# Batched matrix product on one core: transposes in two pieces a half, and two-bank copies in the last group

## The chip, the cores and the metric

The kernel runs on one core of one Trainium2 chip. The time is that of one execution on the device in microseconds (us); less is better. The engines that matter are TensorE (PE, the matrix products; PEld is its weight load), VectorE (DVE), ScalarE (ACT), GpSimd (POOL) and SyncE (SP), which here only issues transfers. The transfers themselves run on 16 DMA engines.

## The reference

```
x: 32 x 256 x 512, y: 32 x 512 x 384, float32
out[b] = x[b] @ y[b]          # 32 products of 256x512 by 512x384, float32 out
```

## The kernel before

**Groups and halves.** The 32 batches are taken four at a time (Q = 4), which makes N = 8 groups, numbered 0 to 7. Each of the four batches of a group has 32 of the 128 partitions (PQ = 32). x of a group is loaded as `x_sb` (two buffers), y as `y_sb` (two buffers). The 256 rows of a product are cut into two halves (NE = 2, index e) of 128 rows, and the sum over the 512 columns of x into T = 16 steps of 32. A chunk is STEP = 4 of these steps, so a half has NC = 4 chunks.

**SP** issues all transfers in one queue (lines 75 and 98 to 111). Two groups are loaded at once at the start; after that x of group n waits until POOL has cast both halves of group n - 2, and y of group n until POOL has cast the first half of x of group n - 1 (`s_cast`). The output of all groups stays in `o_sb` and goes out by three stores at the end: groups 0 to 4 (issued behind the last load, when group 5 is in its second half), groups 5 and 6 (when group 7's second half has done its first chunk), and group 7, which waits for ACT's and DVE's last copies (lines 107 to 109).

**POOL** casts to 16 bit, x a half at a time into `x_r` (`round_x`, line 121) and y in pieces into `y_r` (`round_y`, line 130). `x_r` and `y_r` have one buffer each. The cast of a half of x of group n waits until DVE has done with the half that it overwrites, which DVE tells with the first of its copies (`s_free`). The cast of a piece of y waits until TensorE has used up that piece of the group before.

**DVE** transposes `x_r` into `xt_sb`, which holds one half (`transpose_x`, line 154: 128 partitions x 256 words for a chunk, each word two 16-bit values). While TensorE computes half (n, e), DVE transposes the next half, chunk by chunk, each as soon as TensorE has used up the same chunk (`chunk_done`, lines 174 to 179). Then it copies 5 of the 16 blocks of the finished half from the accumulators to `o_sb` (`collect`, line 163; a block is 32 partitions x 384 elements, for one batch g and one of H = 4 runs of 32 rows). The loop runs over groups 0 to 6; group 7 is written out behind it (lines 189 to 191).

**ACT** copies the other 11 blocks of each half, bank after bank, each as soon as the bank's last product is done (`scalar_half`, line 195). Groups 0 to 5 are a loop, groups 6 and 7 (STRAIGHT = 2) are written out.

**TensorE** takes, for each half, one token each from `s_act` and `s_dve` (the accumulators of two halves ago are copied out; two tokens of each are there at the start), and at each chunk one from `s_yr` and one from `s_xt`. It then issues 16 products a chunk, 64 a half (lines 231 to 250). The accumulators `o_ps` are 8 PSUM banks, one for each half and batch: bank e x 4 + g.

Of the kernel before, what the change touches and what calls it, by code (L numbers as in the profile page):

```python
# [11 lines left out]
Q = 4  # L12
NE = 2
STEP = 4
STRAIGHT = 2
# [4 lines left out]
def kernel(  # L20
# [9 lines left out]
    _, _, K = y.shape  # L30

    PQ = P // Q
    R = I // PQ
    H = R // NE
    T = J // PQ
    TW = T // 2
    N = B // Q
    NC = T // STEP

    def sbuf(name, shape, dtype):  # L40
        return nc.alloc_sbuf_tensor(name, shape, dtype).ap()
# [3 lines left out]
    o_sb = sbuf("o_sb", [P, N, NE, H, K], F32)  # L45
# [4 lines left out]
    o_ps = nc.alloc_psum_tensor("o_ps", [P, NE * Q, 512], F32).ap()  # L50
# [7 lines left out]
    s_act = nc.alloc_semaphore("s_act")  # L58
    s_dve = nc.alloc_semaphore("s_dve")
    s_pe = nc.alloc_semaphore("s_pe")  # L60
# [24 lines left out]
    def bank_done(n, e, g):  # L85
        return (n * NE + e) * MARKS + NC + g

    def chunk_done(n, e, a):
        return (n * NE + e) * MARKS + (a + 1 if a < NC - 1 else MARKS)
# [57 lines left out]


    v = nc.vector
    AW = STEP // 2  # L150
    words = x_r.bitcast(F32).rearrange("p e h (q t) -> p e t h q", t=TW)
    xt_w = xt_sb.rearrange("p t (h s) -> p t h s", s=PQ)

    def transpose_x(e, a):
        w = slice(a * AW, (a + 1) * AW)
        v.transpose(xt_w[:, w], words[:, e, w]).then_inc(s_xt, 1)  # L156
# [3 lines left out]
    BLOCKS = [(g, h) for g in range(Q) for h in range(H)]  # L160
    OWN = 5

    def collect(copy, n, e, blocks, first=None, last=None):
        for i, (g, h) in enumerate(blocks):
            ins = copy(  # L165
                o_sb[g * PQ : (g + 1) * PQ, n, e, h],
                o_ps[h * PQ : (h + 1) * PQ, e * Q + g, :K],
            )
            if i == 0 and first is not None:
                ins.then_inc(first, 1)  # L170
            if i == len(blocks) - 1 and last is not None:
                ins.then_inc(last, 1)

    def vector_half(n, e):
        for a in range(NC):
            v.wait_ge(s_pe, chunk_done(n, e, a))
            if a == 0:
                v.wait_ge(s_cast, NE * n + e + 2)
            transpose_x(1 - e, a)
        collect(v.tensor_copy, n, e, BLOCKS[-OWN:], s_free, s_dve)  # L180

    v.sem_inc(s_dve, NE)
    v.wait_ge(s_cast, 1)
    for a in range(NC):
        transpose_x(0, a)
    with v.Fori(0, N - 1) as n:
        for e in range(NE):
            vector_half(n, e)
    vector_half(N - 1, 0)
    v.wait_ge(s_pe, chunk_done(N - 1, 1, NC - 1))  # L190
    collect(v.tensor_copy, N - 1, 1, BLOCKS[-OWN:], None, s_dve)

    a_ = nc.scalar

    def scalar_half(n, e):
        for g in range(Q - 1):
            a_.wait_ge(s_pe, bank_done(n, e, g))
            blocks = [b for b in BLOCKS[:-OWN] if b[0] == g]
            collect(a_.copy, n, e, blocks, None, s_act if g == Q - 2 else None)
# [4 lines left out]
    with a_.Fori(0, N - STRAIGHT) as n:  # L204
        with a_.Fori(0, NE) as e:
            scalar_half(n, e)
    for n in range(N - STRAIGHT, N):
        for e in range(NE):
            scalar_half(n, e)

    te = nc.tensor

    def take(sem):
        te.wait_op(sem, 1, "sem-ge").then_inc(sem, -1)  # L214

    def product(ps, w, m, start, stop, g):
        return te.add_instruction(  # L217
            mybir.InstMatmult(
                name=nc.get_next_instruction_name(),
                start_tensor_calc=start,  # L220
                stop_tensor_calc=stop,
                tile_size=(PQ, P),
                tile_position=(PQ * g, 0),
                engine=mybir.EngineType.PE,
                ins=[te.lower_ap(m), te.lower_ap(w)],
                outs=[te.lower_ap(ps)],
            )
        )

    xt = xt_sb.bitcast(MM_DT).rearrange("p t (m c) -> p t m c", c=2)  # L230
    with te.Fori(0, N):
        with te.Fori(0, NE) as e:
            take(s_act)
            take(s_dve)
            for t in range(T):
                if t % STEP == 0:
                    take(s_yr)
                    take(s_xt)
                for g in range(Q):
                    s = slice(g * PQ, (g + 1) * PQ)  # L240
                    ins = product(
                        o_ps[:, e * Q + g, :K],
                        xt[s, t // 2, :, t % 2],
                        y_r[s, t],
                        t == 0,
                        t == T - 1,
                        g,
                    )
                    if t == T - 1 or (g == Q - 1 and t % STEP == STEP - 1):
                        ins.then_inc(s_pe, 1)  # L250
# [30 lines left out]
```

## Time and profile before

| What | us |
|---|---|
| median of three runs | 132.0 (131.89 to 132.18) |
| the profiled execution's own time | 132.13 |
| its span, first to last instruction | 130.8 |
| busy in the span: PE, PEld | 61.4, 46.7 |
| busy in the span: DVE, ACT, POOL | 82.7, 84.1, 74.2 |

The profiled execution took 1.3 us more than its span, which lies before the first instruction and behind the last one. HBM was read for 41.94 MB and written for 12.58 MB.

How to read the views quoted below. A row of groups has the line, engine, operation, out<-in with shapes and count, then busy us and mean ns of one, then the idle time ahead of it and what ended most of that. A row of the timeline has start and length in us, the engine, the line, the operation and a count; consecutive instructions of one kind are merged, and the idle time ahead of the first stands in brackets. SPq rows are issues of transfers. A row of stretches has the stretch, its length, the busy time and instruction count of PE, PEld, DVE, ACT and POOL, then the clock granted to TensorE, the mean share of 16 DMA engines and GB/s. A row of issues has the count, KB each and the time from issue to landing. In the row of DMA slices each digit is the busy share of one of 40 equal slices in tenths, 9 for 90% or more. A row of waits has total us, count and the longest.

### The profile page before, as it was taken

The numbers are of one execution on the slowest core, as the hardware profiler recorded it, in microseconds if no ns is written. First come the engines' busy times: TensorE is split into PE (matmuls) and PEld (weight loads), VectorE is DVE, ScalarE is ACT, GpSimd is POOL, SyncE is SP. The second block draws the span as 40 slices with busy tenths as digits, with TensorE's granted clock in tenths as the row PEclk, the third lists the DMA queues.
The fourth block names the chain that finished last, engine by engine and source line by source line (L and its number), as shares of the span: only waits on it lengthen the run. The fifth ranks groups of instructions, "written<-read, shape, count | busy, mean of one in ns | idle before, by whom it ended". The sixth has DMA issues, their size and how long they took to land. (4 is left out here: it accounts for less than half of the span.)

```text
span 130.8 us, 3199 instructions
## 1 busy us (share of the span) xinstructions
PE 61.4 (47%) x1024; PEld 46.7 (36%) x1024; DVE 82.7 (63%) x144; ACT 84.1 (64%) x178; POOL 74.2 (57%) x42
## 2 busy tenths in 40 slices
PE   0000009910992589089329905980975499100000
PEld 0000009800991566046129604970953236000000
DVE  0000036899379999985997997599999957920000
ACT  0400000599659989993998899399999957994000
POOL 0006991199929965992899459758973970000000
PEclk9999999995589689977986985599599959965555
DMA  5999999999999999999999999999999999999995
GB/s 120 451 396 441 421 431 451 443 408 428 451 413 421 438 443 401 436 436 443 423 458 398 443 408 466 398 418 436 463 398 408 427 438 425 436 428 421 425 440 248
DMA packets 3379, 54.55 MB, mean 417 GB/s; under 512 B 304, under 2 KB 304, under 8 KB 304
## 3 DMA queue, kind: packets, MB, share of 16 engines
q1 hardware_dynamic: 3376, 54.53, 98.1%
q14 instruction: 3, 0.02, 0.0%
HBM read 41.94 MB, written 12.58 MB: 417 GB/s over the span
## 5 line engine op out<-in xcount | busy, mean ns | idle before, releaser
L165 ACT COPY o_sb<-o_ps (+1 forms) x176 | 82.6, 469 | 31.7 <-PE o_ps L217 29.6
L217 PE MATMUL o_ps<-y_r,xt_sb 32*128 32x384 f16 x1024 | 61.4, 384 | 50.4 <-PEq L214 49.5
L217 PEld LDWEIGHTS o_ps<-y_r,xt_sb 32*128 32x128 f16 x1024 | 46.7, 107 | 64.6 <-issue 56.8
L156 DVE STREAM_TRANSPOSE xt_sb<-x_r 128x256 f32<-128x256 f32 x64 | 38.1, 626 | 30.9 <-POOL x_r L126 18.4
L136 POOL CAST y_r<-y_sb 128x1536 f16<-128x1536 f32 (+1 forms) x22 | 44.3, 2049 | 15.8 <-DMA y_sb<-in_y_dram 15.3
L165 DVE COPY o_sb<-o_ps 32x384 f32 (+1 forms) x80 | 44.6, 557 | 1.6
L126 POOL CAST x_r<-x_sb 128x2048 f16<-128x2048 f32 x16 | 30.2, 1893 | 16.8 <-DVE o_sb L165 12.1
L202 ACT ACT_TABLE_LOAD x1 | 1.3, 1283 | 3.4 <-PEq L78 3.4
L265 POOL MEMSET const-float32-0.0<- 128x1 f32 x1 | 0.1, 98 | 0.2 <-issue 0.2
L202 ACT COPY spare<-const-float32-0.0 1x1 f32<-1x1 f32 x1 | 0.2, 190 | 0.0
L265 POOL MEMSET const-bfloat16-1.0<- 128x1 bf16 x1 | 0.1, 101 | 0.0
L265 POOL MEMSET const-uint8-127<- 128x1 uint8 x1 | 0.1, 101 | 0.0
L265 POOL MEMSET const-float32-1.0<- 128x1 f32 x1 | 0.1, 98 | 0.0
## 6 DMA issues: line engine op xcount, KB each, us to landing
y_sb<-in_y_dram SPq DMA_DIRECT2D x8, 3072.0 KB, 16.8
x_sb<-in_x_dram SPq DMA_DIRECT2D x8, 2048.0 KB, 17.0
out_dram<-o_sb SPq DMA_DIRECT2D x1, 7680.0 KB, 33.9
out_dram<-o_sb SPq DMA_DIRECT2D x1, 3072.0 KB, 17.3
out_dram<-o_sb SPq DMA_DIRECT2D x1, 1536.0 KB, 11.5
```

The source lines that it names most:

```text
L126: po.tensor_copy(x_r[:, e], x_sb[n % 2][:, e * H : (e + 1) * H]).then_inc(s_cast, 1)
L136: ins = po.tensor_copy(y_r[:, s], y_sb[n % 2][:, s])
L156: v.transpose(xt_w[:, w], words[:, e, w]).then_inc(s_xt, 1)
L165: ins = copy(o_sb[g * PQ : (g + 1) * PQ, n, e, h], o_ps[h * PQ : (h + 1) * PQ, e * Q + g, :K],)
L202: a_.copy(spare, nc.const_aps.tensor(0.0, [1, 1], F32))
L217: return te.add_instruction(mybir.InstMatmult(name=nc.get_next_instruction_name(), start_tensor_calc=start, stop_tensor_calc=stop, tile_si ...
L265: nc = _bacc.Bacc("TRN2", target_bir_lowering=False, num_devices=1)
```

## The change

The transposes of a half are made in PT = 2 pieces of two chunks each (AW is doubled), so a piece waits for the second of its two chunks, and TensorE takes `s_xt` twice a half instead of four times. The accumulators change places: bank g x 2 + e instead of e x 4 + g, so the two halves of one batch lie in neighbouring banks. In group 7, ACT and DVE copy a block of both halves by one instruction (`collect_last`), when the second half's bank is done; the copies of group 7's first half that ran while the second half was computed are gone. ACT's straight part is then group 6 by `scalar_half` and group 7 by `collect_last`.

```diff
-    AW = STEP // 2
+    PT = 2
+    AW = TW // PT
...
-                o_ps[h * PQ : (h + 1) * PQ, e * Q + g, :K],
+                o_ps[h * PQ : (h + 1) * PQ, g * NE + e, :K],
...
-    def vector_half(n, e):
-        for a in range(NC):
-            v.wait_ge(s_pe, chunk_done(n, e, a))
+    def collect_last(copy, blocks, last=None):
+        for i, (g, h) in enumerate(blocks):
+            ins = copy(
+                o_sb[g * PQ : (g + 1) * PQ, N - 1, :, h],
+                o_ps[h * PQ : (h + 1) * PQ, g * NE : (g + 1) * NE, :K],
+            )
+            if i == len(blocks) - 1 and last is not None:
+                ins.then_inc(last, NE)
+
+    def transpose_half(n, e):
+        for a in range(PT):
+            v.wait_ge(s_pe, chunk_done(n, e, (a + 1) * NC // PT - 1))
             if a == 0:
                 v.wait_ge(s_cast, NE * n + e + 2)
             transpose_x(1 - e, a)
+
+    def vector_half(n, e):
+        transpose_half(n, e)
         collect(v.tensor_copy, n, e, BLOCKS[-OWN:], s_free, s_dve)
...
-    for a in range(NC):
+    for a in range(PT):
         transpose_x(0, a)
...
-    vector_half(N - 1, 0)
+    transpose_half(N - 1, 0)
     v.wait_ge(s_pe, chunk_done(N - 1, 1, NC - 1))
-    collect(v.tensor_copy, N - 1, 1, BLOCKS[-OWN:], None, s_dve)
+    collect_last(v.tensor_copy, BLOCKS[-OWN:], s_dve)
...
-    for n in range(N - STRAIGHT, N):
+    for n in range(N - STRAIGHT, N - 1):
         for e in range(NE):
             scalar_half(n, e)
+    for g in range(Q - 1):
+        a_.wait_ge(s_pe, bank_done(N - 1, NE - 1, g))
+        blocks = [b for b in BLOCKS[:-OWN] if b[0] == g]
+        collect_last(a_.copy, blocks, s_act if g == Q - 2 else None)
...
                 if t % STEP == 0:
                     take(s_yr)
+                if t % (T // PT) == 0:
                     take(s_xt)
...
-                        o_ps[:, e * Q + g, :K],
+                        o_ps[:, g * NE + e, :K],
```

## The prediction

> **What bounds it now.** I read the page from the top: the share of each engine, then the DMA row of the slices, the chain that ended last, the costliest groups, the DMA issues.
>
> ```profile
> span 130.8 us, 3199 instructions
> ...
> DMA  5999999999999999999999999999999999999995
> ...
> DMA packets 3379, 54.55 MB, mean 417 GB/s; under 512 B 304, under 2 KB 304, under 8 KB 304
> ...
> ACT o_sb L165 8%; PE o_ps L217 2%
> ...
> L165 ACT COPY o_sb<-o_ps (+1 forms) x176 | 82.6, 469 | 31.7 <-PE o_ps L217 29.6
> L156 DVE STREAM_TRANSPOSE xt_sb<-x_r 128x256 f32<-128x256 f32 x64 | 38.1, 626 | 30.9 <-POOL x_r L126 18.4
> L165 DVE COPY o_sb<-o_ps 32x384 f32 (+1 forms) x80 | 44.6, 557 | 1.6
> L202 ACT COPY spare<-const-float32-0.0 1x1 f32<-1x1 f32 x1 | 0.2, 190 | 0.0
> ...
> y_sb<-in_y_dram SPq DMA_DIRECT2D x8, 3072.0 KB, 16.8
> x_sb<-in_x_dram SPq DMA_DIRECT2D x8, 2048.0 KB, 17.0
> out_dram<-o_sb SPq DMA_DIRECT2D x1, 7680.0 KB, 33.9
> out_dram<-o_sb SPq DMA_DIRECT2D x1, 3072.0 KB, 17.3
> out_dram<-o_sb SPq DMA_DIRECT2D x1, 1536.0 KB, 11.5
> ```
>
> No engine is above two thirds of the span, but the DMA row is 9 in all slices but the first and the last: the transfers run from start to end without a hole. The chain of waits says something else: it ends in ACT's copies (8%) and the store behind them, which takes 11.5 us to land. To choose between the two I cut the span into stretches at the two issues that matter, the third load of y and the last store.
>
> ```profile
> 0.00:3.00 3.00, 0.00 (x0) 0.00 (x0) 0.00 (x0) 0.00 (x0) 0.20 (x4) 1.00 0.57 131
> 3.00:27.46 24.46, 7.41 (x128) 6.29 (x128) 7.33 (x13) 4.65 (x9) 11.29 (x8) 1.00 0.99 424
> 27.46:119.30 91.84, 53.97 (x896) 40.46 (x896) 75.36 (x132) 79.45 (x170) 62.67 (x31) 0.81 1.00 429
> 119.30:126.00 6.70, 0.00 (x0) 0.00 (x0) 0.00 (x0) 0.00 (x0) 0.00 (x0) 0.50 1.01 433
> 126.00:130.80 4.80, 0.00 (x0) 0.00 (x0) 0.00 (x0) 0.00 (x0) 0.00 (x0) 0.50 0.72 307
> ```
>
> The last two columns are the DMA share and GB/s. From 3 us to 126 us the share is 0.99 to 1.01. At 119.3 us, when the last store is issued, 433 x 6.7 + 307 x 4.8 = 2.90 + 1.47 = 4.37 MB are still to move; the last store is 1536 KB = 1.57 MB of that, so 2.80 MB, or 6.5 us at 430 GB/s, stand in the queue ahead of it. Its 11.5 us are mostly waiting in line. The kernel is bound by its 54.5 MB; the copies at the end are early.
>
> **How early.** The issues, from the timeline of SP's queue and of the last stage:
>
> ```profile
> 0.74 0.39 SPq L73 DMA_DIRECT2D y_sb<-in_y_dram  x1
> ...
> 105.92 5.82 PE L217 MATMUL o_ps<-y_r,xt_sb 32*128 32x384 f16 x96 [0.31 <-PEq L214]
> ...
> 108.56 2.78 PEld L217 LDWEIGHTS o_ps<-y_r,xt_sb 32*128 32x128 f16 x64 [0.47 <-issue]
> 108.66 10.59 ACT L165 COPY o_sb<-o_ps 32x384 f32<-32x384 f32 x22 [2.22 <-PE o_ps L217]
> ...
> 109.44 5.73 DVE L165 COPY o_sb<-o_ps 32x384 f32<-32x384 f32 x10
> ...
> 119.27 0.34 SPq L96 DMA_DIRECT2D out_dram<-o_sb  x1
> ```
>
> The first load is issued at 0.74 us, and the 0.39 MB of the first 3 us are 0.93 us of flow, so bytes start about 1.3 us after an issue. The last store is harmless as long as it is issued before 119.3 + 6.5 - 1.3 = 124.5 us: 5.2 us of slack.
>
> **Edit 1: group 7's copies (ACT's and DVE's end).** Removed on ACT: the 22 copies of 384 elements that run from 108.66 to 119.25, half of them while TensorE still computes the second half. Added: 11 copies of 2 x 384 elements, which wait for both halves, so they start when TensorE ends, 105.92 + 5.82 = 111.7 us. No row shows a copy over two banks. Bounds: it can't take less than one half's 469 ns, and as two separate instructions it would take 2 x 469 = 938 ns. Between them, the 1x1 copy gives ACT's fixed part as about 190 ns; (469 - 190) / 383 = 0.73 ns an element, so 190 + 767 x 0.73 = 749 ns. I take 749, the value that both rows give, plus the 12 ns between copies (10.59 / 22 = 0.481 us a step): 11 x 0.761 = 8.4 us, ACT ends at 120.1 us, 0.85 us later than the 119.25 of now. By the bounds, 11 x 0.481 = 5.3 us gives 117.0 and 11 x 0.95 = 10.5 us gives 122.2. All of it is before 124.5: the cost is nothing, and what hides it is the 2.80 MB of earlier stores in the queue. Only a copy above (124.5 - 111.7) / 11 = 1.16 us would show.
>
> The Trainium skill, page ScalarE: Activation LUTs, section What ACT_TABLE_LOAD costs, gives 186 ns + 0.833 ns per element for an ACTIVATE with immediate operands. At 384 elements that would be 506 ns, and the trace has 469, so the measured slope is lower; by the page a two-bank copy would be an estimated 826 ns, ACT would end at 120.9 us, and the total would stay the same.
>
> DVE's 10 copies of 557 ns become 5, each between 0.557 and 1.114 us. They start behind TensorE's end at 111.7 and finish by 117.4 at the latest, ahead of ACT in every combination with its middle value. Which bank a half's products go to (g x 2 + e for e x 4 + g) changes an address alone; nothing is added, and the row that it would show in is the matmuls' duration. I take zero; a matmul slowed by a tenth would put the 2.8 us of the last half at 3.1.
>
> **Edit 2: transposes in two pieces.** 64 transposes of 256 elements become 32 of 512. A single one takes 626 ns; the rows below have four back to back in 2.22 us (555 each) and two in 1.29. So one of 512 lies between 0.65 (all of it fixed) and 1.29 us (none); I take 1.1, two of the back-to-back steps, since the row of four is the nearest to a longer stream. The instruction count on DVE falls, its time little. What moves is when: the second piece waits for the last matmul of a half, and DVE's copies, whose first releases the cast of the next x on POOL, are queued behind it. TensorE's first take of a half waits for a piece twice as long.
>
> ```profile
> 18.44 2.22 DVE L156 STREAM_TRANSPOSE xt_sb<-x_r 128x256 f32<-128x256 f32 x4 [18.44 <-POOL x_r L126]
> 19.38 7.41 PE L217 MATMUL o_ps<-y_r,xt_sb 32*128 32x384 f16 x128 [19.38 <-PEq L214]
> ...
> 23.52 1.29 DVE L156 STREAM_TRANSPOSE xt_sb<-x_r 128x256 f32<-128x256 f32 x2 [0.33 <-PE o_ps L217]
> 24.21 5.77 ACT L165 COPY o_sb<-o_ps  x12 [19.28 <-PE o_ps L217]
> 24.84 2.85 DVE L165 COPY o_sb<-o_ps 32x384 f32 x5
> 25.54 3.73 POOL L126 CAST x_r<-x_sb 128x2048 f16<-128x2048 f32 x2 [5.30 <-DVE o_sb L165]
> 27.46 0.33 SPq L73 DMA_DIRECT2D y_sb<-in_y_dram  x1
> ```
>
> The place where this could reach the DMA queue is the thinnest one, early: the third y load is issued at 27.46, when the first of POOL's two casts ends, which waited for DVE's first copy. By then two y and three x loads, 12.58 MB, have been issued, and 131 x 3 + 424 x 24.46 = 0.39 + 10.37 = 10.76 MB moved. 1.82 MB are queued, 4.2 us, less 1.3 us of start: 2.9 us of slack. The change delays it by up to 0.65 us at the start (the first piece ahead of TensorE) and by the second piece: half 0 ends at about 24.2 where ACT's first copy starts, 24.8 with the late start, the piece lasts 0.65 to 1.29 us, and DVE's first copy starts at 25.4 to 26.1 instead of 24.84. That is 0.6 to 1.25 us late, inside 2.9. Cost: nothing; if that cover were gone, about 1 us.
>
> In the loop the second piece is also needed by TensorE at the middle of the next half, 2.78 / 2 = 1.4 us after the half ends at full clock; a piece of 1.1 us plus its wait just fits, and with 1.29 us TensorE would stall some 0.1 us a half. Whether compute keeps up:
>
> ```profile
> 32.42 7.65 PE L217 MATMUL o_ps<-y_r,xt_sb 32*128 32x384 f16 x128 [5.62 <-PEq L214]
> ...
> 43.85 4.48 PE L217 MATMUL o_ps<-y_r,xt_sb 32*128 32x384 f16 x64 [3.78 <-PEq L214]
> ```
>
> and from the view of waits:
>
> ```profile
> POOL y_r L136 <- DMA y_sb<-in_y_dram: 15.3, 5, 10.4
> ```
>
> From group 1 to group 2 TensorE took 43.85 - 32.42 = 11.43 us, a group's loads (3072 + 2048 KB = 5.24 MB at 429 GB/s) 12.2. Adding at most 0.65 us for a late first copy gives 12.1, still under the transfers; and later POOL is found waiting for y to land (15.3 us in five waits, of which the longest is one of 10.4), so compute has caught up with the DMA. Removed waits and instructions gain nothing either, for the same reason.
>
> **Sum.** Edit 1: 0, edit 2: 0, on 130.8 us of span and 132.13 us for the profiled execution. The median of the three runs is 132.0 us, 0.13 lower, and the forecast goes by it: **132.0 us**, within 0.2% (0.26 us, about what a measurement of this kernel can tell from no change) of before. Its own range is that of the runs of before and a little more, 131.8 to 132.3.
>
> **Rivals.** (a) Slower: the last store's 11.5 us go along with its issue, as the chain of waits reads. The copies start only at 111.7, so ACT ends 0.85 us later and the kernel with it: 132.9 us (135.0 with copies of 938 ns, 129.8 with copies of 469). For it: the chain. Against it: 1.57 MB at 430 GB/s are 3.7 us, and the DMA share is 1.01 just behind the issue. It decides once the last issue comes after 124.5 us. Chance 0.07. (b) Slower: the loads come late in the middle. Place: the third y load; price: what its delay, two pieces less the 1.25 us that one small and two small ones take there now, exceeds 2.9 us by. It decides from a 512-element transpose of (2.9 + 1.25) / 2 = 2.1 us, where the bound is 1.29; at 2.5 us the time would be 2 x 2.5 - 1.25 - 2.9 = 0.85 us longer, 132.9 us. Against it: both transpose rows. Chance 0.03. (c) Faster by the end of a single DMA engine:
>
> ```profile
> 129.00:129.50 0.50, 0.00 (x0) 0.00 (x0) 0.00 (x0) 0.00 (x0) 0.00 (x0) 0.50 0.75 320
> 129.50:130.00 0.50, 0.00 (x0) 0.00 (x0) 0.00 (x0) 0.00 (x0) 0.00 (x0) 0.50 0.07 25
> ```
>
> and the queues from 99 to 107 us:
>
> ```profile
> q1 hardware_dynamic: 274, 3.37, 99.5%
> q14 instruction: 3, 0.02, 0.7%
> ```
>
> From 129.5 us on the share is 0.07, which is one engine of 16: one ends up to 0.5 us behind the rest. And the second row of the queues has three fetches of instructions, 0.7% of 16 engines in 8 us, 0.9 us in all, 0.3 us each, on engines that carry the stores. They fall where ACT and DVE run their straight last part, which the change shortens (11 copies fewer on ACT, some ten instructions fewer on DVE). A fetch that disappears from the engine that ends last gives 0.3 to 0.5 us: 131.6 us. For it: these rows; against it: nothing shows that the late engine is one of those, or that the code falls under a boundary. Chance 0.11. The Trainium skill, page Runtime: NRT & Kernel Launch, section Instruction fetch mechanics, calls the cost of crossing a fetch boundary "mostly hidden", with 16 KiB blocks; the row's 0.02 MB for three is nearer to 8 KB each. By that page (c) would be worth nothing. (d) The change doesn't do what it says, because a two-bank copy takes as long as two: ACT ends at 122.2 us, still 132.0; it is part of the forecast.
>
> **How the numbers follow.** Forecast 0.79, (a) 0.07, (b) 0.03, (c) 0.11. That makes faster 0.11, same 0.79, slower 0.10. The range must reach a little past the likeliest case's own 131.8 to 132.3: down to (c)'s 131.6, up to 132.9 for (a) at its middle value.
>
> **What would show it.** The DMA row stays 9 from the second slice to the last but one, with as many MB. ACT's last stage has 11 copies of two halves at about 0.75 us, begins near 111.7 and ends near 120; the last store then lands in about 10.7 us instead of 11.5, because it waits less in line: that is the sharpest sign, since (a) has it at 11.5 again. Transposes: 32, about 1.1 us each. The third y load is issued near 28.4. The number of instruction fetches and the share past 129.5 us decide (c). The forecast is wrong if the DMA row shows a hole, if copies over two banks take over 1.16 us, or if packets themselves take longer, for which nothing here speaks.

## The result and the profile after

The changed kernel is a little slower: 132.47 us median (131.96 to 133.27, 20 runs) against 132.03 us (131.82 to 132.42, 20 runs), ratio 1.0039 with a 95% interval of 1.0027 to 1.0052. The forecast was no difference, 132.0 us. The runs of the changed kernel spread about twice as wide as those of before, 1.31 against 0.60 us: 6 of 20 lie under 132.2 us, 8 over 132.8.

The page of the changed kernel, the lines that answer to those shown of before (`collect` is now at line 166, `collect_last` at 178, the transposes at 157):

```profile
span 131.6 us, 3091 instructions
...
DMA  4999999999999999999999999999999999999994
...
DMA packets 3378, 54.54 MB, mean 414 GB/s; under 512 B 304, under 2 KB 304, under 8 KB 304
...
q14 instruction: 2, 0.02, 0.0%
...
ACT o_sb L178 7%; PE o_ps L235 4%
...
L166 ACT COPY o_sb<-o_ps (+1 forms) x154 | 72.4, 470 | 32.4 <-PE o_ps L235 30.6
L157 DVE STREAM_TRANSPOSE xt_sb<-x_r 128x512 f32<-128x512 f32 x32 | 34.5, 1097 | 36.8 <-POOL x_r L126 18.5
L178 ACT COPY o_sb<-o_ps 32x768 f32<-32x768 f32 x11 | 8.7, 790 | 3.9 <-PE o_ps L235 3.8
L178 DVE COPY o_sb<-o_ps 32x768 f32<-32x768 f32 x5 | 4.8, 957 | 2.2 <-PE o_ps L235 2.1
...
out_dram<-o_sb SPq DMA_DIRECT2D x1, 1536.0 KB, 9.1
```

The new instructions cost what was expected or nearly: 1097 ns for a transpose (1.1 us taken), 790 ns for a two-bank copy on ACT (749), 957 on DVE (0.557 to 1.114). The bytes are the same. Even the DMA row of the slices looks as full as before, and that is the trap of this case: a slice is 3.3 us, and its digit says 9 from 90% on. In stretches of 1 us, where the transfers of x and y of group 2 meet, first the changed kernel, then the one before (last two columns: DMA share, GB/s):

```profile
31.00:32.00 1.00, 0.00 (x0) 0.00 (x0) 0.97 (x2) 0.98 (x3) 1.00 (x2) 0.92 1.32 492
32.00:33.00 1.00, 0.00 (x0) 0.00 (x0) 0.96 (x3) 0.98 (x3) 1.00 (x1) 0.50 0.76 295
33.00:34.00 1.00, 0.00 (x0) 0.00 (x0) 0.97 (x3) 0.98 (x3) 1.00 (x2) 0.50 1.09 418
```

```profile
31.00:32.00 1.00, 0.00 (x0) 0.00 (x0) 0.97 (x3) 0.98 (x3) 1.00 (x2) 0.50 1.36 582
32.00:33.00 1.00, 0.58 (x7) 0.49 (x11) 0.81 (x2) 0.98 (x3) 1.00 (x1) 0.50 1.03 442
```

From 32 to 33 us 295 GB/s flow instead of 442 (a share over 1 in one of these stretches comes from counting a packet where it starts). By the packet records four of the 16 DMA engines had run out of packets. (These records do not name the engine; where a packet starts as another ends, both are taken as one engine's.) It is not made up later: every transfer lands in 16 shares, one of each engine, and the late ones stay late. The end of the changed kernel shows it:

```profile
129.50:130.00 0.50, 0.00 (x0) 0.00 (x0) 0.00 (x0) 0.00 (x0) 0.00 (x0) 0.50 0.46 197
130.00:130.50 0.50, 0.00 (x0) 0.00 (x0) 0.00 (x0) 0.00 (x0) 0.00 (x0) 0.50 0.23 98
130.50:131.00 0.50, 0.00 (x0) 0.00 (x0) 0.00 (x0) 0.00 (x0) 0.00 (x0) 0.50 0.12 49
```

The share falls in steps, 0.46, 0.23, 0.12: the engines end one after another. In the semaphore records of the two traces the 16 shares of the last store land between 129.74 and 131.60 us here, where before 15 of them land between 129.60 and 130.28 and the last at 130.77. The kernel is as long as its last engine: the last share lands 0.83 us later, and the span is 0.8 us longer. The engines fell apart in one transfer: the shares of group 2's y land between 39.43 and 40.10 us before, and between 39.65 and 41.48 us after, a spread of 0.67 and of 1.83 us. In the transfer just ahead of it, x of group 2, the spread is still 0.67 and 0.87.

Why that transfer was late is in the timeline of the changed kernel:

```profile
18.53 2.10 DVE L157 STREAM_TRANSPOSE xt_sb<-x_r 128x512 f32<-128x512 f32 x2 [18.53 <-POOL x_r L126]
...
19.94 8.23 PE L235 MATMUL o_ps<-y_r,xt_sb 32*128 32x384 f16 x128 [19.94 <-PEq L232]
...
25.43 1.12 DVE L157 STREAM_TRANSPOSE xt_sb<-x_r 128x512 f32<-128x512 f32 x1 [1.11 <-PE o_ps L235]
25.54 10.60 ACT L166 COPY o_sb<-o_ps  x22 [20.53 <-PE o_ps L235]
26.57 2.85 DVE L166 COPY o_sb<-o_ps 32x384 f32 x5
...
27.27 3.73 POOL L126 CAST x_r<-x_sb 128x2048 f16<-128x2048 f32 x2 [6.94 <-DVE o_sb L166]
29.19 0.33 SPq L73 DMA_DIRECT2D y_sb<-in_y_dram  x1
```

The third load of y is issued at 29.19 us, where it was 27.46: 1.73 us later. TensorE starts 19.94 - 19.38 = 0.56 later, behind the longer first piece. ACT's first copy, at the end of the half, comes 25.54 - 19.94 = 5.60 us after that start, before it was 24.21 - 19.38 = 4.83: 0.77. DVE's first copy comes 1.03 us after ACT's instead of 0.63, behind the longer second piece: 0.40. Sum 1.73.

### The profile page after: what moved, and what is told of

Its sections match the earlier page's. It is cut to its first block, busy times and chain, and to the rows that moved or that the text cites. A ratio compares the mean times of both kernels' runs of the same rounds, so it can differ in the third digit from the quotient of the medians.

```text
span 131.6 us, 3091 instructions
## 1 busy us (share of the span) xinstructions
PE 65.6 (50%) x1024; PEld 52.7 (40%) x1024; DVE 78.2 (59%) x107; ACT 82.6 (63%) x167; POOL 73.9 (56%) x42
## 5 line engine op out<-in xcount | busy, mean ns | idle before, releaser
L166 ACT COPY o_sb<-o_ps (+1 forms) x154 | 72.4, 470 | 32.4 <-PE o_ps L235 30.6
L235 PE MATMUL o_ps<-y_r,xt_sb 32*128 32x384 f16 x1024 | 65.6, 408 | 48.2 <-PEq L232 45.0
L235 PEld LDWEIGHTS o_ps<-y_r,xt_sb 32*128 32x128 f16 x1024 | 52.7, 114 | 60.7 <-issue 54.2
L157 DVE STREAM_TRANSPOSE xt_sb<-x_r 128x512 f32<-128x512 f32 x32 | 34.5, 1097 | 36.8 <-POOL x_r L126 18.5
L166 DVE COPY o_sb<-o_ps 32x384 f32 x70 | 39.0, 557 | 1.5
L178 ACT COPY o_sb<-o_ps 32x768 f32<-32x768 f32 x11 | 8.7, 790 | 3.9 <-PE o_ps L235 3.8
L178 DVE COPY o_sb<-o_ps 32x768 f32<-32x768 f32 x5 | 4.8, 957 | 2.2 <-PE o_ps L235 2.1
```

What stands on the lines that cost most here:

```text
L166: ins = copy(o_sb[g * PQ : (g + 1) * PQ, n, e, h], o_ps[h * PQ : (h + 1) * PQ, g * NE + e, :K],)
L178: ins = copy(o_sb[g * PQ : (g + 1) * PQ, N - 1, :, h], o_ps[h * PQ : (h + 1) * PQ, g * NE : (g + 1) * NE, :K],)
L235: return te.add_instruction(mybir.InstMatmult(name=nc.get_next_instruction_name(), start_tensor_calc=start, stop_tensor_calc=stop, tile_si ...
```

## The experiments

The theory after the result, Q: the DMA queue comes short at the third load of y, because two-piece transposes hold back its issue; nothing else of the change costs time. Rival C: the later copies of group 7 and the later last store. Rival F: single DMA engines delayed by chance of the code's layout (instruction fetches), as (c) of the prediction. (The changed kernel's trace has two such fetches within its span, of 0.31 us each, at 102.89 and 105.19 us, none near 32 us.) Ratios are to the kernel before, beside which each ran.

**The pieces alone.**

```diff
-    AW = STEP // 2
+    PT = 2
+    AW = TW // PT
...
-        for a in range(NC):
-            v.wait_ge(s_pe, chunk_done(n, e, a))
+        for a in range(PT):
+            v.wait_ge(s_pe, chunk_done(n, e, (a + 1) * NC // PT - 1))
...
                     take(s_yr)
+                if t % (T // PT) == 0:
                     take(s_xt)
```

> The kernel before with the transposes in two pieces and nothing else (old banks, old copies of group 7). Theory Q (the DMA queue runs short at the third load of y, because two-piece transposes make its issue late): the issue at 28.5 to 29.5 us instead of 27.46, a dip of GB/s between 31 and 34 us, total as with the whole change, 1.002 to 1.006 of before. Rival C (the two-bank copies and the later last store cost the time): no difference, 0.999 to 1.001. Rival F (instruction fetches or slow packets on one DMA engine, by chance of code layout): no sign forecast; the third y load and the time need not go together.

132.73 us (132.56 to 133.39), ratio 1.0063 [1.0043, 1.0083]. Third y load at 29.42 us, 369 and 344 GB/s in the two us from 32 on:

```profile
29.42 0.33 SPq L73 DMA_DIRECT2D y_sb<-in_y_dram  x1
```

```profile
32.00:33.00 1.00, 0.00 (x0) 0.00 (x0) 0.95 (x3) 0.98 (x3) 1.00 (x1) 0.68 1.02 369
33.00:34.00 1.00, 0.00 (x0) 0.00 (x0) 0.99 (x2) 0.98 (x3) 1.00 (x2) 0.50 0.86 344
```

As Q has it, and a little more. But of the difference about 0.4 us lies outside the span: in all 6 runs the time is 1.68 to 1.77 us over the span, in those of before 1.28 to 1.37. By spans it is 131.0 against 130.6 us (medians).

**The copies alone**, the changed kernel with four pieces again.

```diff
-    PT = 2
+    PT = 4
```

> The whole change except that the transposes stay in four pieces: new banks and two-bank copies in group 7. Theory Q: third y load issued near 27.5 us as before, no dip between 31 and 34 us, ratio 0.999 to 1.001 although ACT ends some 2 us later than before. Rival C: as slow as the whole change, 1.003 to 1.005.

132.09 us, ratio 1.0006 [0.9997, 1.0015]. Rival C falls. Early and late rows of its timeline:

```profile
19.57 8.20 PE L235 MATMUL o_ps<-y_r,xt_sb 32*128 32x384 f16 x128 [19.57 <-PEq L232]
...
25.27 10.61 ACT L166 COPY o_sb<-o_ps  x22 [20.34 <-PE o_ps L235]
...
28.50 0.33 SPq L73 DMA_DIRECT2D y_sb<-in_y_dram  x1
...
109.85 10.98 SPq L96 DMA_DIRECT2D out_dram<-o_sb  x2
111.66 8.81 ACT L178 COPY o_sb<-o_ps 32x768 f32<-32x768 f32 x11 [4.38 <-PE o_ps L235]
```

ACT starts at 111.66 and ends at 120.47, the last store follows, 1.2 us later than before, at no cost. The third row is a surprise: with four pieces, too, the third y load can be as late as 28.50, since the first half lasted 25.27 - 19.57 = 5.70 us here. It still came in time:

```profile
32.00:33.00 1.00, 0.00 (x0) 0.00 (x0) 0.97 (x3) 0.96 (x4) 1.00 (x2) 0.50 1.03 442
```

It was only just in time: by the packet records one engine ran out and stood idle for 0.04 us until its first packet of this load started at 31.66 us, 3.2 us after the issue.

**The whole change, with the load early.**

```diff
-        sp.wait_ge(s_cast, NE * (n - 1) + 1)
+        if n > 2:
+            sp.wait_ge(s_cast, NE * (n - 1) + 1)
         load_y(n)
```

> The whole change, but SP issues the third load of y (group 2) right behind the third load of x, when both casts of group 0's x are done, instead of waiting for the first cast of group 1's x as well; no other wait differs. Theory Q: issue near 20.8 us, no dip, the spread of the DMA engines' ends back to that of before, ratio to before 0.997 to 1.001 (131.7 to 132.1 us). Rivals C and F: still 1.003 to 1.005, since all else of the change is there.

132.09 us, ratio 1.0011 [1.0002, 1.0020], spread 131.94 to 132.36. Issue at 20.73 us; nothing else of the changed kernel is touched, and the loss goes but for 0.1%. ACT's last copies end at 121.53 us, 2.3 us later than before, so Rival C fails here too. Two stretches of it:

```profile
32.00:33.00 1.00, 0.00 (x0) 0.00 (x0) 0.97 (x3) 0.98 (x3) 1.00 (x1) 0.50 0.97 418
```

```profile
129.50:130.00 0.50, 0.00 (x0) 0.00 (x0) 0.00 (x0) 0.00 (x0) 0.00 (x0) 0.50 0.07 25
```

**The kernel before, with the load late.**

```diff
-        sp.wait_ge(s_cast, NE * (n - 1) + 1)
+        sp.wait_ge(s_cast, NE * (n - 1) + (2 if n == 2 else 1))
```

> The kernel before; only SP's third load of y waits for the second cast of group 1's x instead of the first, 1.8 us later by the trace (29.3 us instead of 27.46). No engine's program but SP's changes. Theory Q: a dip between 31 and 34 us and 1.003 to 1.007 of before. Rivals C and F: 0.999 to 1.001, since four pieces, old copies and old code layout are kept.

132.70 us, ratio 1.0054 [1.0035, 1.0073]. The delay alone, in SP's program alone, costs as much as the whole change. It is a longer delay, though: the issue came at 30.40 us, where 29.3 was expected and the changed kernel has 29.19. With this run rival F falls as the main cause. Its dip has the same size:

```profile
30.40 0.33 SPq L73 DMA_DIRECT2D y_sb<-in_y_dram  x1
```

```profile
32.00:33.00 1.00, 0.00 (x0) 0.00 (x0) 0.97 (x3) 0.98 (x3) 1.00 (x1) 0.50 0.77 295
```

**A still later load, on an empty queue**, to see how the loss grows with the delay (the dose).

```diff
         sp.wait_ge(s_cast, NE * (n - 1) + 1)
+        if n == 2:
+            sp.wait_ge(s_pe, chunk_done(1, 0, 0))
```

> The kernel before; SP's third load of y also waits for the first chunk of group 1, which TensorE ends near 33.8 us, so it is issued when all that came before has landed (32.0 to 32.9 us). It measures the start-up of a transfer on an empty queue, and the dose. Theory Q with the start-up of the prediction, 1.3 us: bytes from 35.1 us on, 2.2 to 3.1 us of every DMA engine lost, 134.5 to 135.2 us. With a start-up of nearly 4 us, as the last engine of the whole change seems to have had: about 137 us. Rivals C and F: no change.

137.64 us, ratio 1.0398 [1.0349, 1.0446]. The issue came at 35.58 us, later than the 33.8 assumed.

```profile
35.58 0.33 SPq L73 DMA_DIRECT2D y_sb<-in_y_dram  x1
```

```profile
33.00:34.00 1.00, 0.37 (x3) 0.30 (x3) 0.99 (x2) 0.98 (x3) 1.00 (x2) 0.50 0.00 0
34.00:36.00 2.00, 2.00 (x30) 1.98 (x29) 0.42 (x2) 1.95 (x5) 2.00 (x2) 0.50 0.00 0
36.00:37.00 1.00, 1.00 (x19) 0.94 (x15) 0.46 (x2) 0.01 (x1) 1.00 (x1) 0.50 1.64 393
```

By the packet records all 16 engines take up the load between 36.54 and 36.87 us, 0.96 to 1.29 us after the issue: on an empty queue the 1.3 us of the prediction were right. They had stood idle for 3.8 to 5.4 us, 4.8 in the mean, and each one's first packet then took 1.3 to 2.2 us instead of 0.91. The span grew by 5.6 us (136.3 for 130.7, medians): the gap and about 0.7 us for starting again. The Trainium skill, page DMA: Bandwidth & Descriptors, section Specifications, gives a first-byte latency of about 0.6 us for this path. Counted from the end of the issue, which takes 0.33 us, the first engine's packet starts after 0.63 us, which agrees, and the last engine's after 0.96.

**The kernel before, with the load early**, by the edit of the third experiment, run twice.

> The kernel before; SP's third load of y waits only for both casts of group 0's x and is issued right behind the third load of x, near 20.7 us. Theory Q: the queue never came short before, so at most the odd late run goes; 0.998 to 1.000 of before. If before, too, lost something there in most runs: 0.995 to 0.998.

> The kernel before with its third load of y issued right behind the third load of x, once more, for a narrower interval. Theory Q: 0.998 to 1.000; what it can gain is the odd run in which the kernel before came short, and no more, since all the bytes still have to move.

131.96 us, ratio 0.9984 [0.9967, 1.0000], and 131.92 us, ratio 1.0000 [0.9990, 1.0010]. It has the lowest median of all versions, but is not measurably better than before. Its runs spread less than those of before beside it, 131.81 to 132.09 in the second set, where before had 131.78 to 132.60; but the 25 runs of before beside the first experiments, 131.77 to 132.15, spread little wider, so that the early load narrows the runs is not shown. That the odd late runs of before are short queues too is only argued; no such run was profiled.

**Which piece.** Two kernels of before with part of edit 2: the very first half in two pieces, or all halves but that one.

```diff
+    def transpose_two(e, a):
+        w = slice(a * 2 * AW, (a + 1) * 2 * AW)
+        v.transpose(xt_w[:, w], words[:, e, w]).then_inc(s_xt, 2)
```

> The kernel before; only the very first half's transposes, ahead of TensorE's start, are in two pieces (each gives TensorE two tokens). Theory Q: TensorE starts 0.5 us later, the third y load is issued 0.5 us later than in the kernel before at the same ramp of TensorE, 28.0 to 29.0 us; the queue comes short from somewhere between 28.5 and 29.2 us, so 1.000 to 1.003 of before. If the first piece were the whole cause: 1.003 to 1.006.

> The kernel before; the transposes of every half but the very first in two pieces (each gives TensorE two tokens), the first half's in four as before. Theory Q: TensorE starts as before, DVE's first copy comes 0.5 us later, the third y load at 28.0 to 29.0 us, 1.000 to 1.003 of before, less than both parts together (1.004 by the whole change). If the loop's later pieces cost by themselves, in each of 16 halves, apart from the third y load: 1.003 or more with no dip between 31 and 34 us.

1.0025 [1.0005, 1.0044] and 1.0029 [1.0009, 1.0049]. By these middles either part alone does more than half of the damage; the intervals leave that open, but neither part is free. The runs fall in two lots: 5 of 12 and 4 of 12 at 131.80 to 132.06 us, the others at 132.33 to 133.01. The profiled executions are of the low lots (132.06 and 131.81 us), with issues at 28.32 and 27.74 us (28.0 to 29.0 was expected of both) and no dip; what the higher lots looked like is not in a profile. Two lots are what a threshold would give where the issue varies from run to run by more than either part moves it; that is argued, not shown.

**The pieces alone, with the load early.**

> Two-piece transposes alone, with the third load of y issued right behind the third load of x. Theory Q: 0.999 to 1.001; where the whole change with the early load kept 0.0011, this tells whether the rest belongs to the pieces (again 1.001) or to the copies (1.000). Rival F: as the pieces alone, 1.004 to 1.008.

132.53 us, ratio 1.0029 [1.0011, 1.0046], so not as Q said. But the span's median is 130.8 us against 130.7, and the queue has no dip; all of it is the time outside the span, 1.71 to 1.77 us as with the pieces alone. The whole change has 1.29 to 1.40, like before. What it is remains open; it belongs to these two programs, not to the change.

**TensorE warmed up.** 96 products that no output uses, ahead of the first half, unrolled or as a loop, in the changed kernel.

```diff
+    te.wait_ge(s_yr, 1)
+    for i in range(96):
+        g = i % Q
+        s = slice(g * PQ, (g + 1) * PQ)
+        product(o_ps[:, g * NE, :K], y_r[s, 0, :P], y_r[s, 0], True, True, g)
```

> The whole change, with 96 products added that TensorE computes from 12.4 us on, from the first cast piece of y, into a bank that is overwritten later (no output depends on them). They are there so that TensorE's first half runs at 321 ns a product and not at 512 to 522. Theory Q: the first half then lasts 2.6 to 3.3 us instead of 5.1, the third y load is issued at 27.0 to 27.7 us instead of 29.2, no dip between 31 and 34 us, ratio 0.999 to 1.002. Rivals C and F: 1.003 to 1.005, or more for the added work.

> As after_warm, but the 96 added products are a loop of 24 times 4, so TensorE's program hardly grows. after_warm issued the third y load at 27.13 us and had no dip between 31 and 34 us, yet lost time at another place: a gap of up to 0.4 us between the first and second group's transfers near 20 us on some DMA engines. If the longer program did that: the gap goes and the ratio is 0.999 to 1.002. If the added products do it: 1.004 to 1.007 again.

Unrolled: issue at 27.13 us, as wanted, 418 GB/s from 32 to 33 us, and yet 132.91 us, ratio 1.0056 [1.0038, 1.0074], by the time alone what rivals C and F had forecast. It lost time at another place, between x of group 1 and y of group 1, whose load had been issued at 2.12 us:

```profile
21.00:22.00 1.00, 1.00 (x32) 0.75 (x27) 0.00 (x0) 0.00 (x0) 0.00 (x0) 1.00 0.85 369
```

The loop was to say whether the longer program did it, but its products took longer (9.35 us for the 96 instead of 5.38), so that TensorE's real first half began at 23.0 us, which put the issue off to 30.01 us, and the time to 133.83 us, ratio 1.0138 [1.0115, 1.0161]. That is another late load that costs.

What made the gap near 20 us stands in the unrolled kernel's trace, as a queue of instruction fetches that no other run has (a row of the page, with packets, MB and share):

```profile
q8 instruction: 1, 0.02, 0.0%
```

This one packet of 16 KB ran from 19.70 to 20.71 us, where an engine would have begun y of group 1. That engine's first packet of y then took 1.41 us instead of 0.91, and its share of that load landed 1.4 us late; the other 15 lost nothing. At the end of this execution the last share lands 0.59 us behind the next one (131.26 and 130.67 us). So in this kernel, whose TensorE program had been made longer, an instruction fetch did what rival F had in mind. The loop has no such fetch, and none of its engines was late there; that the fetch is TensorE's own is not shown otherwise.

## Why the prediction was wrong

**What bounds the kernel** was right: the queue, not the chain of waits. The last store was issued at 122.50 us in the changed kernel, 3.2 us later than before, and landed in 9.1 us instead of 11.5. Rival (a) is refuted by that, and by the copies alone at 1.0006. Rival (c) got its sign and not its gain: the changed kernel has two fetches of instructions within its span instead of three, and is not faster.

**Edit 1** was right in its cost of nothing and near in its sizes. The 749 ns on ACT came near the 790 by two errors that partly cancel: by the two copies measured, 469 and 790 ns, an element costs (790 - 469) / 384 = 0.836 ns and the fixed part is 148 ns. It was the fixed part that was lower than 190, and not the slope that was lower than 0.833, as the prediction read it. ACT ended at 122.5 instead of 120.1, 2.0 us of that because TensorE ended later (the copies start at 113.67 us instead of 111.7) and 0.4 us because they took longer, still in time.

**Edit 2** is the step that failed: "That is 0.6 to 1.25 us late, inside 2.9. Cost: nothing". The thinnest place and the chain of causes to it were the right ones, and rival (b), with a chance of 0.03, is what happened, though not by its condition, a transpose of over 2.1 us; the slack was sized too large, and the delay was counted from one execution that happened to be early.

*The delay* was 1.73 us between the two profiled executions. The two pieces gave 0.56 + 0.40 = 0.96, inside the 0.6 to 1.25. The rest, 0.77, is the length of TensorE's first half, which I took as fixed. Its products take 492 to 523 ns at first and drop to 321 at some moment. The rows of one us, in the changed kernel

```profile
23.00:24.00 1.00, 1.00 (x19) 1.00 (x15) 0.78 (x1) 0.00 (x0) 0.00 (x0) 1.00 0.97 418
24.00:25.00 1.00, 1.00 (x20) 1.00 (x14) 0.32 (x1) 0.00 (x0) 0.00 (x0) 1.00 1.08 467
```

and in the one before

```profile
23.00:24.00 1.00, 1.00 (x29) 0.93 (x20) 0.68 (x2) 0.00 (x0) 0.00 (x0) 1.00 0.91 393
```

have 19 and 20 products a us at a time when before has 29. The first product under 400 ns starts at 22.96 us before, 3.6 us after TensorE's start, and at 24.99 us in the changed kernel, 5.0 us after it; over all twelve profiles of kernels without added products it is 2.9 to 6.1 us. It isn't the change that does this: the copies alone, with four pieces, had a first half of 5.70 us, the kernel before with the late load 25.16 - 19.54 = 5.62. So the third y load of before may come anywhere from 27.46 to 28.5 us at least, and one profiled execution showed the early end of it. In the mean the change delays less: DVE's first copy starts at 24.84 to 26.06 us in the six profiles with four pieces throughout, 25.60 in the mean, and at 26.04 to 26.80 us in the four with two pieces throughout, 26.37 in the mean. That is 0.77 us, inside the forecast; the one profile of before at hand was an early one.

What changes at that moment is the granted clock, though its column stands at 1.00 in all these rows. The trace's records of the clock begin only at 23.02 us before and at 25.01 us in the changed kernel, with full clock; ahead of that the column has no record to go by. In all 14 traces the first record lies 0.03 to 0.16 us behind the first product under 400 ns. The Trainium skill, page TensorE: Matmul & The Clock Gate, section What's actually happening, says that TensorE runs at half clock until it was busy for a window of about 3.4 us, and that the windows run freely, without regard to the kernel's start. The traces agree in kind: but for the last one of each trace, the clock's records are 3.41 us long or a multiple of it, and the products speed up 2.9 to 6.1 us after TensorE's start, the shortest a little under one such window. By that page the length of the first half could have been expected to vary, and the prediction should have had it as a term of the delay.

*The slack*, 2.9 us, was too large. An issue at 28.50 us brought no dip, one at 29.19 did: the queue bears 1.0 to 1.7 us more than the 27.46 of before, not 2.9. The bytes ahead of it were counted rightly (4.2 us from 27.46 is 31.7, and the first engine took up group 2's y at 31.65). The term that was too small is the start-up of 1.3 us. It holds on an empty queue. Behind other transfers it was longer for some engines: 3.2 us for the one that just ran out with the copies alone, which leaves 4.2 - 3.2 = 1.0 us of slack. In the changed kernel, issued at 29.19, the last engine's first packet started at 33.62, 4.4 us later, after at least 1.3 us of idling. The first packets were slow as well: of the 16, twelve took 1.06 to 1.55 us instead of 0.91, and one 1.90, nine of these 13 on engines that had not stood idle. Why some engines get a load so much later than others isn't shown by any run here. What is shown is that the mean over 16 engines is the wrong measure: the kernel pays for the one that runs out longest.

**Whether compute keeps up**, and the TensorE wait in the loop, were answered rightly: with the load early the whole change costs 0.1%, and the pieces alone, by the span, as little. TensorE does end later with the whole change and the early load, at 112.83 us instead of 111.74, and the queue hides it.

## What to carry to other kernels

In a kernel bound by its transfers, a change on any engine is free only as long as every load is still issued in time; look for the issue with the least queued ahead of it, follow what releases it, and take off the measured slack whatever varies from run to run, such as the slow start of the first products. A DMA row that is full in slices of 3 us doesn't show that no engine ran dry: look at stretches of 1 us around that issue, and at how far apart the engines end. Where a load waits for more than its buffer needs, as group 2's y did here for a cast that doesn't read it, issuing it early takes the sensitivity away, even where it gains nothing by itself.

## What the runs showed of the hardware that was not expected

- A load that comes when its queue is almost empty loses more than the gaps: an engine's first packet of 24 KB takes up to 1.9 us instead of 0.91, on engines without a gap too, and 1.3 to 2.2 us after a long one.
- The delay of an engine stays to the end: the spread of 1.83 us at 41 us of the changed kernel is 1.86 us at its end (129.74 to 131.60).
- One fetch of 16 KB of instructions takes 1.0 us of one DMA engine; that engine landed its share of the load behind it 1.4 us late.
- Two programs that differ in the code of their engines alone can differ by 0.4 us outside the span (1.72 against 1.33 us), in every run.
- A late load costs differently from kernel to kernel: 0.7 us of time for an issue at 30.40, 1.8 us for one at 30.01 in the warmed-up loop, where a single engine ended 1.8 us behind the others.
